# A softmax over relative-position-biased logits on one core: two reciprocals per chunk, and stores issued behind two exps of the next chunk

## Chip, core and metric

The kernel runs on one core of one Trainium2 chip. The metric is the device time of one execution in microseconds (us). Three executions of the kernel before took 1333.96, 1325.47 and 1325.87 us; the median is 1325.87 us.

## What is computed

The logits are a float32 array of 2 x 8 x 2112 x 2112, so there are 33,792 rows of 2112 numbers. To each row a bias is added that depends only on the head and on the distance of the two positions, clipped to 16 either way. Then each row goes through a softmax with its own maximum taken off.

```python
def reference(logits, rel_bias):          # (2, 8, 2112, 2112), (8, 33)
    rel = pos[:, None] - pos[None, :]
    rel_clipped = np.clip(rel, -16, 16) + 16
    logits = logits + rel_bias[:, rel_clipped][None]
    logits = logits - logits.max(axis=-1, keepdims=True)
    exp = np.exp(logits)
    return exp / exp.sum(axis=-1, keepdims=True)
```

## The kernel before

One partition of the 128 holds 132 consecutive rows of one batch. The work is cut into **chunks** of R = 6 rows per partition (128 x 12672 floats, one load and one store of 6336 KB each), and four chunks make a **round**: chunks 0 and 1 are twelve rows of the first batch, chunks 2 and 3 the same twelve of the second. There are K = 11 rounds, so 44 chunks. Four buffers `X[0]` to `X[3]` in on-chip memory hold one chunk each; chunk m of every round uses `X[m]`, and all work on it is done in place. In this document chunk (k, m) is chunk m of round k, counted from 0.

Each of three engines runs its own list of instructions in the order in which it is written, without a scheduler, and they meet at semaphores:

- **SP** issues the loads (`load`, L90-L91). The four loads of round 0 go at once. The load of chunk (k+1, m) waits at L88 until the store of chunk (k, m) has landed (`st[m]`), since it goes into the same buffer.
- **DVE** copies a window of the bias table once per round (L172). For each chunk it waits for the load (`ld[m]`), then adds the bias to each of the six rows and takes the negated maximum in the same instruction (`add`, L186; each is followed by a short read of the accumulator, which signals `added`). Then it runs `scale` (L207-L213): it waits until all six exps are done (`expd`), forms six reciprocals of the sums in one instruction (L210, which signals `inv`), waits for it, and multiplies the first DV = 4 rows (L213, each signals `scaled`).
- **ACT** runs the six exps of a chunk (`exps`, L192-L200; ACTIVATE at L197, each after its own `added`, and a read of the accumulator behind it, which signals `expd`). Then `scale_rest` (L215-L220) waits for `inv` and multiplies the last two rows (L218). Then `store` (L93-L95) waits until all six rows are scaled and issues the store of the chunk.

So loads go out on SP's queue and stores on ACT's queue, both to the same set of 16 DMA engines. On ACT a store stands behind all of its own chunk's work and ahead of the next chunk's exps. The helper `take` (L87-L88) waits for a semaphore to reach n and takes n off; it is a row of its own in the trace at L88 (EVENT_SEMAPHORE). Where an instruction only waits (`wait_ge`), the wait is part of that instruction.

Of the kernel before, what the change touches and what calls it, by code (L numbers as in the profile page):

```python
# [15 lines left out]
def kernel(  # L16
# [6 lines left out]
    nc = tc.nc  # L23
# [10 lines left out]
    NBUF = 4  # L34
    R = 6
# [3 lines left out]
    assert K * G == RP  # L39
    SW = S + G - 1  # L40
    DV = 4

    io = ctx.enter_context(tc.tile_pool(name="io", bufs=1))
    X = [io.tile([P, R * S], FP32, tag=f"X{b}", name=f"X{b}") for b in range(NBUF)]
# [5 lines left out]
    tot = io.tile([P, NBUF * R], FP32, tag="tot", name="tot")  # L50
    rec = io.tile([P, NBUF * R], FP32, tag="rec", name="rec")
# [15 lines left out]
    def view(t, offset, dims):  # L67
        return bass.AP(tensor=t.tensor, offset=t.offset + offset, ap=[[list(t.ap[0])[0], P]] + dims)

    def rows(t, k, m):  # L70
        return bass.AP(
            tensor=t.tensor, offset=t.offset + (m // M) * (H * S * S) + (m % M) * R * S + k * (G * S), ap=[[RP * S, P], [1, R * S]],
        )

    with tc.tile_critical(no_gpsimd_drain=True):  # L75
# [3 lines left out]
        expd = nc.alloc_semaphore("expd")  # L79
        scaled = nc.alloc_semaphore("scaled")  # L80
        inv = nc.alloc_semaphore("inv")
        rb = nc.alloc_semaphore("rb")
        zero = nc.alloc_semaphore("zero")
        idx = nc.alloc_semaphore("idx")
# [2 lines left out]
        def take(eng, sem, n):  # L87
            eng.wait_ge(sem, n).then_inc(sem, -n)  # L88
# [4 lines left out]
        def store(k, m):  # L93
            take(nc.scalar, scaled, R)
            nc.scalar.dma_start(out=rows(out, k, m), in_=X[m][:, :]).then_inc(st[m], 16)  # L95
# [10 lines left out]
        v = nc.vector  # L106
# [6 lines left out]
        def settle():  # L113
# [9 lines left out]
            out=bass.AP(tensor=F2.tensor, offset=F2.offset, ap=[[Q * step, P // Q], [1, H * W]]),  # L123
            in_=bass.AP(tensor=rel_bias.tensor, offset=rel_bias.offset, ap=[[0, P // Q], [1, H * W]]),
# [15 lines left out]
        for o, n, s, op in ((eq, NB, q, ALU.is_equal), (lt, NB, q, ALU.is_lt), (hsel, H, h, ALU.is_equal),  # L140
# [24 lines left out]
                           in_=view(reg, 1, [[1, NB - 1], [0, RP - W]])))  # L165
# [9 lines left out]
        def row(m, i):  # L175
            return X[m][:, i * S : (i + 1) * S]

        def col(t, m, i, n=1):
            c = m * R + i
            return t[:, c : c + n]  # L180
# [7 lines left out]
                    scale=-1.0, scalar=BIG, op0=ALU.add, op1=ALU.min, accum_out=col(nmax, m, i),  # L188
                ).then_inc(added, 1)

        def exps(m):
            for i in range(R):  # L192
                if i < R - 1:
                    nc.scalar.wait_ge(added, i + 1)
                else:
                    take(nc.scalar, added, R)
                nc.scalar.activation(  # L197
                    out=row(m, i), in_=row(m, i), func=ACTF.Exp, scale=-1.0, bias=col(nmax, m, i),
                    accum_out=col(tot, m, i),
                ).then_inc(expd, 1)  # L200

        def scales_begin(eng, m):
            if m < NBUF - 1:
                eng.wait_ge(inv, m + 1)
            else:
                take(eng, inv, NBUF)

        def scale(m):
            take(v, expd, R)
            v.reciprocal(out=col(rec, m, 0, R), in_=col(tot, m, 0, R)).then_inc(inv, 1 if m < NBUF - 1 else NBUF + 1)  # L210
            scales_begin(v, m)
            for i in range(DV):
                v.tensor_scalar_mul(out=row(m, i), in0=row(m, i), scalar1=col(rec, m, i)).then_inc(scaled, 1)  # L213

        def scale_rest(m):  # L215
            scales_begin(nc.scalar, m)
            for i in range(DV, R):
                nc.scalar.activation(  # L218
                    out=row(m, i), in_=row(m, i), func=ACTF.Copy, scale=col(rec, m, i),
                ).then_inc(scaled, 1)  # L220

        with nc.Fori(0, K, 1, engines=[ENG.DVE]) as k:  # L222
            window(k)
            for m in range(NBUF):
                add(m)
                scale(m)
        with nc.Fori(0, K, 1, engines=[ENG.Activation]) as k:
            for m in range(NBUF):
                exps(m)
                scale_rest(m)  # L230
                store(k, m)

# [28 lines left out]
```

## Time and profile before

| | before |
|---|---|
| median of three executions | 1325.87 us (1325.47 to 1333.96) |
| span of the profiled execution, first to last instruction | 1323.8 us |
| median less the span | 2.1 us |
| DVE busy, ACT busy | 866.2 us (65%), 757.2 us (57%) |
| bytes moved by DMA, mean rate over the span | 570.98 MB, 431 GB/s |
| queue of the loads (q1), queue of the stores (q10), share of 16 DMA engines | 50.0%, 49.8% |

The span is what the profiler recorded of one execution; no time of its own outside the span is given for that execution, so the 2.1 us are the difference to the median of the three. The page has a line for each engine with its busy time, a strip of 40 slices in which the DMA row tells how busy the 16 DMA engines were (9 is 90% or more), and the queues with their bytes. "Issue to landing" is the time from the instruction that starts a transfer to the last of its completion signals; it holds the time in which the transfer stands in a queue. A row of the timeline gives start, duration, engine, line and operation; in square brackets stands how long the engine idled before it, and what ended that. "DVEq" or "ACTq" is the part of an engine that handles waits and issues transfers. A transfer's end is seen as small packets of under 512 bytes, one from each of the 16 DMA engines.

### The profile page before, as it was taken

The page shows a single profiled execution, that of the slowest core. Times are in us where ns is not written, and L with a number is a line of the kernel's source. Part 1 is how long each engine was busy: PE and PEld are TensorE (multiplying, and loading weights), DVE is VectorE, ACT ScalarE, POOL GpSimd, SP SyncE. Part 2 cuts the span into 40 slices and gives each one's busy share as a digit, 9 for nine tenths or more (in the row PEclk, how much of TensorE's full clock was granted, in tenths as well). Part 3 has the DMA queues.
Part 4 walks back from the last instruction along what each step waited for, and adds up shares of the span by engine and source line. Part 5 has one row for each costly group of instructions (what it writes and reads, how often), then busy time and mean ns, then how long its engine had stood idle before and what let it go on. Part 6 is the DMA issues. An engine that isn't in the chain of part 4 may idle for free. (4 is left out here: it accounts for less than half of the span.)

```text
span 1323.8 us, 2109 instructions
## 1 busy us (share of the span) xinstructions
DVE 866.2 (65%) x781; ACT 757.2 (57%) x627; POOL 0.4 (0%) x6
## 2 busy tenths in 40 slices
DVE  6886666566766675576667666556766576566662
ACT  3776655556666555555656555555666565555663
POOL 0000000000000000000000000000000000000000
DMA  9999999999999999999999999999999999999998
GB/s 417 417 423 435 441 435 423 441 438 421 440 441 427 430 441 435 424 440 438 424 437 440 437 423 440 440 421 438 441 432 426 441 437 423 440 440 423 437 441 369
DMA packets 12682, 570.98 MB, mean 431 GB/s; under 512 B 1412, under 2 KB 1416, under 8 KB 1416
## 3 DMA queue, kind: packets, MB, share of 16 engines
q1 hardware_dynamic: 6336, 285.48, 50.0%
q10 hardware_dynamic: 6344, 285.48, 49.8%
q14 instruction: 2, 0.02, 0.0%
HBM read 285.48 MB, written 285.47 MB: 431 GB/s over the span
## 5 line engine op out<-in xcount | busy, mean ns | idle before, releaser
L197 ACT ACTIVATE X<-X,nmax 128x2112 f32<-128x2112 f32 x264 | 542.6, 2055 | 505.1 <-DVE nmax L186 472.4
L186 DVE CUSTOM_DVE_ANT_0 X<-X,F 128x2112 f32<-128x2112 f32 x264 | 605.2, 2354 | 319.1 <-DVEq L88 319.1
L213 DVE TENSOR_SCALAR X<-X,rec 128x2112 f32<-128x2112 f32 x176 | 220.3, 1315 | 2.8
L218 ACT ACTIVATE X<-X,rec 128x2112 f32<-128x2112 f32 x88 | 176.1, 2048 | 17.2 <-DVE rec L210 12.2
L210 DVE RECIPROCAL rec<-tot 128x6 f32<-128x6 f32 x44 | 8.4, 191 | 106.2 <-DVEq L88 106.2
L197 ACT ACTIVATION_READ_ACCUMULATOR X<-X,nmax 128x1 f32 x264 | 49.2, 186 | 0.0
L197 ACT ACT_TABLE_LOAD x11 | 14.1, 1283 | 22.6 <-ACTq L88 19.9
L172 DVE COPY F<-F 128x2123 f32 x11 | 26.0, 2361 | 0.5 <-DVEq L88 0.5
L186 DVE DVE_READ_ACCUMULATOR2_ANT nmax<- 128x1 f32 x264 | 21.6, 82 | 0.0
L144 DVE LOAD_MASK_SELECT F<-F x1 | 0.0, 14 | 6.2 <-DMA F<-in_rel_bias_dram 6.2
L164 DVE COPY F<-own 128x1485 f32<-128x1485 f32 x1 | 1.7, 1698 | 0.0
L120 DVE MEMSET F<- 128x264 f32 x1 | 0.3, 278 | 1.1 <-SPq L75 1.1
L142 DVE TENSOR_SCALAR Z<-rec,Z 128x16 f32<-128x16 f32 (+2 forms) x5 | 0.8, 233 | 0.1
L163 DVE TENSOR_TENSOR F<-F,own 128x528 f32<-128x528 f32 x1 | 0.7, 717 | 0.1
L160 DVE TENSOR_TENSOR F<-Z,own 128x528 f32<-128x528 f32 x1 | 0.7, 705 | 0.0
L150 DVE TENSOR_REDUCE own<-F 128x33 f32<-128x264 f32 x1 | 0.6, 609 | 0.1
L147 DVE TENSOR_TENSOR F<-F,Z 128x264 f32<-128x264 f32 x1 | 0.4, 429 | 0.1
L144 DVE STREAM_SHUFFLE F<-F 128x264 f32<-128x264 f32 x1 | 0.4, 442 | 0.0
L158 DVE SCALAR_TENSOR_TENSOR own<-Z,own 128x16 f32<-128x16 f32 x1 | 0.2, 235 | 0.2 <-DVEq L88 0.2
L155 DVE TENSOR_SCALAR own<-Z,own 128x16 f32<-128x16 f32 x1 | 0.2, 235 | 0.2 <-DVEq L88 0.2
L166 DVE COPY F<-own 128x115 f32<-128x115 f32 x1 | 0.3, 271 | 0.0
L168 DVE COPY F<-own 128x115 f32<-128x115 f32 x1 | 0.3, 271 | 0.0
(11 smaller groups left out, 1.6 us busy)
## 6 DMA issues: line engine op xcount, KB each, us to landing
X<-in_logits_dram SPq DMA_DIRECT2D x44, 6336.0 KB, 38.4
out_dram<-X ACTq DMA_DIRECT2D x44, 6336.0 KB, 59.0
F<-in_rel_bias_dram ACTq DMA_DIRECT2D x1, 4.1 KB
```

The source lines that it names most:

```text
L142: then(v.tensor_scalar(out=o, in0=num[:, 0:n], scalar1=s, scalar2=None, op0=op))
L144: then(v.stream_shuffle(out=T, in_=T, mask=[0] * Q))
L150: then(v.tensor_reduce(out=rbK, in_=view(F2, H * W, [[1, W], [W, H]]), axis=mybir.AxisListType.X, op=ALU.add))
L160: then(v.tensor_tensor(out=bands, in0=view(eq, 0, [[1, NB], [0, W]]), in1=view(rbK, W - 1, [[0, NB], [-1, W]]), op=ALU.mult))
L163: then(v.tensor_tensor(out=bands, in0=bands, in1=view(rest, 0, [[1, NB], [0, W]]), op=ALU.add))
L164: then(v.tensor_copy(out=view(F, C0 + W, [[RP, NB - 1], [1, RP - W]]), in_=view(reg, 1, [[1, NB - 1], [0, RP - W]])))
L172: then(v.tensor_copy(out=F2[:, 0:SW], in_=F[:, bass.ds(RP - G - k * G, SW)]))
L186: v.tensor_tensor_reduce(out=row(m, i), in0=row(m, i), in1=F2[:, x : x + S], scale=-1.0, scalar=BIG, op0=ALU.add, op1=ALU.min, accum_out=c ...
L197: nc.scalar.activation(out=row(m, i), in_=row(m, i), func=ACTF.Exp, scale=-1.0, bias=col(nmax, m, i), accum_out=col(tot, m, i),).then_inc( ...
L210: v.reciprocal(out=col(rec, m, 0, R), in_=col(tot, m, 0, R)).then_inc(inv, 1 if m < NBUF - 1 else NBUF + 1)
L213: v.tensor_scalar_mul(out=row(m, i), in0=row(m, i), scalar1=col(rec, m, i)).then_inc(scaled, 1)
L218: nc.scalar.activation(out=row(m, i), in_=row(m, i), func=ACTF.Copy, scale=col(rec, m, i),).then_inc(scaled, 1)
```

## The change

The change does two things.

The reciprocals are formed in two parts. DVE waits for the first four exps of the chunk (`wait_ge(expd, DV)`), forms four reciprocals, waits for them, and multiplies rows 0 and 1. Then it waits for all six exps, forms the other two reciprocals (signal `inv2`), and multiplies rows 2 and 3. ACT waits for `inv2` in place of `inv`, and multiplies rows 4 and 5 as before.

The store of chunks 0, 1 and 2 of a round moves on ACT behind the first AHEAD = 2 exps of the round's next chunk. The store of chunk 3 stands where it stood, right behind its own chunk's work, ahead of the next round.

```diff
+    AHEAD = 2
...
+        inv2 = nc.alloc_semaphore("inv2")
...
-        def exps(m):
-            for i in range(R):
+        def exps(m, a, b):
+            for i in range(a, b):
...
+        def scale_one(m, i):
+            v.tensor_scalar_mul(out=row(m, i), in0=row(m, i), scalar1=col(rec, m, i)).then_inc(scaled, 1)
 
         def scale(m):
+            v.wait_ge(expd, DV)
+            v.reciprocal(out=col(rec, m, 0, DV), in_=col(tot, m, 0, DV)).then_inc(inv, 1)
+            take(v, inv, 1)
+            for i in range(DV // 2):
+                scale_one(m, i)
             take(v, expd, R)
-            v.reciprocal(out=col(rec, m, 0, R), in_=col(tot, m, 0, R)).then_inc(inv, 1 if m < NBUF - 1 else NBUF + 1)
-            scales_begin(v, m)
-            for i in range(DV):
-                v.tensor_scalar_mul(out=row(m, i), in0=row(m, i), scalar1=col(rec, m, i)).then_inc(scaled, 1)
+            v.reciprocal(out=col(rec, m, DV, R - DV), in_=col(tot, m, DV, R - DV)).then_inc(inv2, 1)
+            for i in range(DV // 2, DV):
+                scale_one(m, i)
 
         def scale_rest(m):
-            scales_begin(nc.scalar, m)
+            take(nc.scalar, inv2, 1)
...
             for m in range(NBUF):
-                exps(m)
+                exps(m, 0, AHEAD)
+                if m:
+                    store(k, m - 1)
+                exps(m, AHEAD, R)
                 scale_rest(m)
-                store(k, m)
+            store(k, NBUF - 1)
```

ACT's list before, from the first chunk's exps on; X_58 is the buffer of chunk 0 and X_59 that of chunk 1, and "ISA [waits scaled]" is the start of the store at L95:

```order
L197 ACTIVATE X_58,tot<-X_58,nmax 128x2112 [waits added] x6
L218 ACTIVATE X_58<-X_58,rec 128x2112 [waits inv]
L218 ACTIVATE X_58<-X_58,rec 128x2112
L95 ISA [waits scaled]
L95 DMA out_dram<-X_58 128x12672
L197 ACTIVATE X_59,tot<-X_59,nmax 128x2112 [waits added] x6
```

The same place after the change:

```order
L199 ACTIVATE X_58,tot<-X_58,nmax 128x2112 [waits added] x6
L221 ACTIVATE X_58<-X_58,rec 128x2112 [waits inv2]
L221 ACTIVATE X_58<-X_58,rec 128x2112
L199 ACTIVATE X_59,tot<-X_59,nmax 128x2112 [waits added] x2
L97 ISA [waits scaled]
L97 DMA out_dram<-X_58 128x12672
L199 ACTIVATE X_59,tot<-X_59,nmax 128x2112 [waits added] x4
```

The store of chunk 0 stands behind two exps that wait for the adds of chunk 1, and so for the load of chunk 1.

DVE's list before, at the end of chunk 0 (its last add, then `scale`, then the first add of chunk 1):

```order
L186 ISA X_58,nmax<-X_58,F_62 128x2112
L186 ISA nmax 128x1
L210 RECIPROCAL rec<-tot 128x6 [waits expd]
L213 TENSOR_SCALAR X_58<-X_58,rec 128x2112 [waits inv]
L213 TENSOR_SCALAR X_58<-X_58,rec 128x2112 x3
L186 ISA X_59,nmax<-X_59,F_62 128x2112 [waits ld1]
```

The same place after the change:

```order
L188 ISA X_58,nmax<-X_58,F_62 128x2112
L188 ISA nmax 128x1
L209 RECIPROCAL rec<-tot 128x4 [waits expd]
L205 TENSOR_SCALAR X_58<-X_58,rec 128x2112 [waits inv]
L205 TENSOR_SCALAR X_58<-X_58,rec 128x2112
L214 RECIPROCAL rec<-tot 128x2 [waits expd]
L205 TENSOR_SCALAR X_58<-X_58,rec 128x2112 x2
L188 ISA X_59,nmax<-X_59,F_62 128x2112 [waits ld1]
```

Two of the four multiplications moved ahead of the wait for the sixth exp, and there is one reciprocal more.

More of the change, by code (lines that the diff above doesn't have):

```diff
@@ L200, in exps @@
                 ).then_inc(expd, 1)
[L202 to L206, printed above, removed]
-        def scale(m):
+        def scale_one(m, i):
+            v.tensor_scalar_mul(out=row(m, i), in0=row(m, i), scalar1=col(rec, m, i)).then_inc(scaled, 1)
+        def scale(m):
+            v.wait_ge(expd, DV)
[3 more added lines that the diff above has]
+                scale_one(m, i)
             take(v, expd, R)
-            v.reciprocal(out=col(rec, m, 0, R), in_=col(tot, m, 0, R)).then_inc(inv, 1 if m < NBUF - 1 else NBUF + 1)
-            scales_begin(v, m)
-            for i in range(DV):
-                v.tensor_scalar_mul(out=row(m, i), in0=row(m, i), scalar1=col(rec, m, i)).then_inc(scaled, 1)
+            v.reciprocal(out=col(rec, m, DV, R - DV), in_=col(tot, m, DV, R - DV)).then_inc(inv2, 1)
+            for i in range(DV // 2, DV):
+                scale_one(m, i)
         def scale_rest(m):
-            scales_begin(nc.scalar, m)
+            take(nc.scalar, inv2, 1)
             for i in range(DV, R):
```

## Prediction

> **What bounds the kernel now.** I read the page's engines and queues first, to see whether any engine is full.
>
> ```profile
> span 1323.8 us, 2109 instructions
> DVE 866.2 (65%) x781; ACT 757.2 (57%) x627; POOL 0.4 (0%) x6
> DMA  9999999999999999999999999999999999999998
> ...
> q1 hardware_dynamic: 6336, 285.48, 50.0%
> q10 hardware_dynamic: 6344, 285.48, 49.8%
> ```
>
> No compute engine is over two thirds busy. The loads (q1) and the stores (q10) fill the 16 DMA engines to 99.8% of the span, in every slice of the strip. Second, the DMA view over windows: the steady part (60 to 1280 us), and the start (2 to 32 us), where only loads run.
>
> ```profile
> DMA packets 11753, 529.45 MB, mean 434 GB/s; under 512 B 1307, under 2 KB 1307, under 8 KB 1307
> ```
> ```profile
> DMA packets 278, 12.88 MB, mean 429 GB/s; under 512 B 20, under 2 KB 24, under 8 KB 24
> q1 hardware_dynamic: 270, 12.87, 100.9%
> ```
>
> The rate is 434 GB/s mixed, and 429 in a short window of loads alone with the engines just as full. So it matters little which queue has work, as long as one has. 570.96 MB (two times 285.48) at 434 GB/s are 1315.6 us. That leaves 8.2 us of 1323.8 in which the DMA engines are not at full rate, most of it at the very start and end. Third, the waits, and for the transfers the time from issue to landing.
>
> ```profile
> ACT X L197 <- DVE nmax L186: 472.4, 44, 17.2
> DVE X L186 <- DVEq L88: 319.1, 42, 8.5
> ```
> ```profile
> L91 SPq DMA_DIRECT2D X<-in_logits_dram x44: 332/333/549, 1.0 to 1244.2; - x44
> ...
> DMA to landing us min/median/max: 17.6/38.4/82.8
> ```
> ```profile
> L95 ACTq DMA_DIRECT2D out_dram<-X x44: 338/339/380, 40.4 to 1303.3; - x44
> ...
> DMA to landing us min/median/max: 19.3/59.0/60.5
> ```
>
> DVE waits some 7.6 us (319.1/42) for each load, and ACT waits behind DVE. The first pair of landing rows is the loads', the second the stores', each with the first and last issue. One transfer at full rate takes 6.488 MB / 434 GB/s = 14.9 us, yet a load takes 38.4 and a store 59.0: the rest is waiting in a queue that is never empty. Last, the timeline of one chunk and the begin of the next:
>
> ```profile
> 145.18 2.36 DVE L186 CUSTOM_DVE_ANT_0 X<-X,F 128x2112 f32<-128x2112 f32 x1 [8.49 <-DVEq L88]
> ...
> 156.37 0.19 ACT L197 ACTIVATION_READ_ACCUMULATOR X<-X,nmax 128x1 f32 x1
> ...
> 158.86 0.08 DVE L186 DVE_READ_ACCUMULATOR2_ANT nmax<- 128x1 f32 x1
> ...
> 161.03 0.19 ACT L197 ACTIVATION_READ_ACCUMULATOR X<-X,nmax 128x1 f32 x1
> 161.36 0.19 DVE L210 RECIPROCAL rec<-tot 128x6 f32<-128x6 f32 x1 [2.42 <-DVEq L88]
> 161.58 4.00 ACT L218 ACTIVATE X<-X,rec 128x2112 f32<-128x2112 f32 x2 [0.37 <-DVE rec L210]
> 161.59 5.01 DVE L213 TENSOR_SCALAR X<-X,rec 128x2112 f32<-128x2112 f32 x4
> ...
> 166.83 0.34 ACTq L95 DMA_DIRECT2D out_dram<-X  x1
> 175.08 2.36 DVE L186 CUSTOM_DVE_ANT_0 X<-X,F 128x2112 f32<-128x2112 f32 x1 [8.49 <-DVEq L88]
> ...
> 177.48 2.06 ACT L197 ACTIVATE X<-X,nmax 128x2112 f32<-128x2112 f32 x1 [11.90 <-DVE nmax L186]
> ...
> 179.76 2.05 ACT L197 ACTIVATE X<-X,nmax 128x2112 f32<-128x2112 f32 x1
> ...
> 181.72 0.19 ACT L197 ACTIVATION_READ_ACCUMULATOR X<-X,nmax 128x1 f32 x1
> ```
>
> A chunk takes 175.08 - 145.18 = 29.90 us, and a load and a store at full rate take 2 x 14.95 = 29.9. The period is the DMA's; compute fills 21.65 of it (145.18 to 166.83). A buffer's round trip is 38.4 + 21.8 + 59.0 = 119.2 us, four periods.
>
> **The change, part by part.** *The reciprocals.* One RECIPROCAL more per chunk costs at most 0.19 us (its row), 44 x 0.19 = 8.4 us of DVE. Its cover is DVE's wait for the next load, 8.49 us in this chunk. The first reciprocal needs four exps, done at 156.37 + 0.19 = 156.6, before DVE's own last add ends at 158.9: its wait is nothing. It runs from about 159.0 and two scales (5.01/4 = 1.25 us each) end at 161.8, after the sixth exp (161.2). Then the second reciprocal, and two scales end at about 164.6, against 166.6 before. ACT's two scales (4.00 us) start some 0.5 us later than 161.58, as they wait for the second reciprocal, and end near 166.1. So the chunk is scaled at 166.1 in place of 166.6: 0.5 us earlier on the way to a store, 2 us earlier on DVE. What DVE gains becomes a longer wait for the load, which the DMA sets: 0 us of the span. Without that cover the extra reciprocals would cost 8.4 us.
>
> *The stores of chunks 0 to 2* (33 of 44). Before, the store goes at 166.83. After, it stands behind two exps of the next chunk, which wait for its load and two adds. No row shows whether ACT issues the store when the second exp starts (179.76) or when it has ended (181.72 + 0.19 = 181.9), so the delay is 12.9 to 15.1 us. The transfer itself is not made longer; I take the delay as hidden, for this reason. The DMA engines run dry only if no buffer has a transfer in a queue. While store m is held back until some 5 to 7 us after load m+1 lands (175.08 to 179.8 or 181.9), the other two buffers' loads or stores are outstanding, and the load that lands next still has most of a period of DMA work ahead of it (loads land 29.90 us apart). In the round trip: 119.2 - 21.8 - 15.1 leaves 82 us for two transfers of 15, so the delay eats 15 of some 52 us of queueing. SP's wait for that store is no later than before, since the store stands that much less long in its queue: from 59.0 to 44 or 46 us. On ACT, the remaining exps now stand behind an issue of 0.34 us whose wait (`scaled`) is long met; ACT idles 11.9 us per chunk. Cost 0.
>
> *The tail* is the one place without other work, since loads have ended there. The last load lands just before the last add, and three stores remain. The rows are the last chunk's, then the landing of the single stores issued at 1243.3, 1273.4 and 1303.3 us, then the packets from 1281.6 to 1289.5 us.
>
> ```profile
> 1243.33 0.34 ACTq L95 DMA_DIRECT2D out_dram<-X  x1
> ...
> 1273.37 0.34 ACTq L95 DMA_DIRECT2D out_dram<-X  x1
> 1281.59 2.36 DVE L186 CUSTOM_DVE_ANT_0 X<-X,F 128x2112 f32<-128x2112 f32 x1 [8.54 <-DVEq L88]
> ...
> 1286.27 2.06 ACT L197 ACTIVATE X<-X,nmax 128x2112 f32<-128x2112 f32 x1
> ```
> ```profile
> out_dram<-X ACTq DMA_DIRECT2D x1, 6336.0 KB, 49.3
> ```
> ```profile
> out_dram<-X ACTq DMA_DIRECT2D x1, 6336.0 KB, 34.3
> ```
> ```profile
> out_dram<-X ACTq DMA_DIRECT2D x1, 6336.0 KB, 19.3
> ```
> ```profile
> DMA packets 64, 3.24 MB, mean 411 GB/s; under 512 B 0, under 2 KB 0, under 8 KB 0
> ```
>
> They land at 1292.6, 1307.7 and 1322.6, 15 us apart: back to back. After the change the store of chunk (10, 2) goes at 1286.3 (start of the second exp) to 1288.4 (its end, and 0.1 for the read) instead of 1273.4. It is late only if the store before it has left the DMA engines by then. At 1289.5 not one of the 16 had finished (no packet under 512 B); the last landed at 1292.6. How long a store takes from issue to its first packet has one case with the other queue full: issued at 40.4, no packet of q10 until 44.7, four by 46. Loads into an empty DMA at the start, issued from 1.0, had 16 packets by 3.0: 2 us at most.
>
> ```profile
> q1 hardware_dynamic: 32, 1.62, 112.0%
> ```
> ```profile
> q10 hardware_dynamic: 4, 0.20, 8.4%
> ```
> ```profile
> q1 hardware_dynamic: 16, 0.81, 120.1%
> ```
>
> So the first packets come between 1286.3 (no start at all) and 1292.7 (1288.4 and 4.3), against engines that come free between 1289.5 and 1292.6. The gap is from 0 to 3.2 us. I take 0: the short start is nearer, since no loads are queued there. The last chunk's own store, 0.5 us earlier than 1303.3, still waits for 1307.7: no gain.
>
> **Sum**: reciprocals 0, delay 0, tail 0 (to +3.2), so 1323.8 + 0 for the span, with the 2.1 us between span and median 1325.9 us, the median of before.
>
> **The rivals.** *The store is not delayed at all.* A wait belongs to the exp itself, and if ACT's sequencer goes on past an exp that still waits, it meets `scaled` and issues the store at about 166.3, where it did before. For it speaks that DVE's sequencer runs ahead of its engine, in the last rows of the chain:
>
> ```profile
> 1298.10 0.17 DVE X L213
> ...
> 1298.30 0.05 DVEq L222
> ...
> 1299.34 3.77 DVE X L213 x3
> ```
>
> The branch at L222 ran at 1298.30, with three scales in front of it still to run. No row shows it passing an instruction whose own wait is unmet. The Trainium skill, Perfetto Trace Analysis, section "Per-instruction lifecycle", says that a DVE or ACT instruction is pushed into a wait queue and the sequencer is then free to fetch the next; by that rule this rival would hold. The time is the same, 1325.9 us, with store landings near 59 us.
>
> *The delay is paid in the ring of buffers* (the other side). If a store's 59 us were its own time and not queueing, SP's wait for `st[m]` would end 13 us later each round, and ten rounds make 130 us: 1456 us. It decides if under 15 of the 52 us of queueing could be given back. Against it: the last store landed 15 us after the one before. The Trainium skill, DMA: Bandwidth & Descriptors, "Rules for kernel authors", advises to issue a DMA early; taken alone it speaks for this rival.
>
> *The tail gap*: 3.2 us, 1329.1 us, if the start takes 4.3 us there too.
>
> *Faster*: at most the 8.2 us outside full rate could go, and no row ties them to the moved instructions.
>
> **Numbers.** About 1% (1312.6 to 1339.1) is what a measurement of this kernel can tell from no change. Delay hidden 0.52, store not delayed 0.28, tail gap 0.10 are all within it: same 0.90. The ring, wholly or in part, is slower: 0.09. Faster 0.01, as 1312.6 is under 1315.6 at full rate. The range runs from 1322, a few us for a run without the small losses, over 1329.1 to 1334, the slowest run of before; only the ring is left out.
>
> **What would show it.** DMA at 434 GB/s from 60 to 1280 us, the chunk period 29.9 us; stores landing in a median of 44 to 46 us (hidden delay) or 59 (not delayed); RECIPROCAL x88, DVE's wait for loads up by about 2 us per chunk; in the tail three stores 15 us apart. A DMA rate under 434 in mid-span, or a period over 30 us, would prove me wrong.

## The result and the profile after

In 22 executions of each, the changed kernel took 1336.37 us (median; 1326.09 to 1338.95) and the kernel before 1327.23 us (1325.30 to 1336.83). The ratio of the comparison is 1.0038, 95% interval 1.002 to 1.0057: some 0.2 to 0.6% slower, within the 1% that was called "same". Median and ratio differ because both kernels have executions near 1326 us and near 1336 us: over 1333 us lie 15 of 22 of the changed kernel and 6 of 22 of before. The profiled execution of the changed kernel took 1336.1 us, with a span of 1334.3 us, and is of the longer sort; that of before (span 1323.8 us) is of the shorter. What follows compares these two, and explains the 10.5 us between them.

The page after, the same lines as those shown of before:

```profile
span 1334.3 us, 2219 instructions
...
DVE 864.5 (65%) x825; ACT 757.2 (57%) x627; POOL 0.4 (0%) x6
...
DMA  9999999999999999999999999999999999999977
...
q1 hardware_dynamic: 6336, 285.48, 49.7%
q10 hardware_dynamic: 6344, 285.48, 49.4%
```

The last two slices of the strip fell to 7: only there are DMA engines visibly idle. In mid-span, 60 to 1280 us, the rate is 433 GB/s against 434:

```profile
DMA packets 11723, 528.54 MB, mean 433 GB/s; under 512 B 1295, under 2 KB 1295, under 8 KB 1295
```

The waits and the two groups of reciprocals:

```profile
DVE X L188 <- DVEq L90: 431.5, 42, 11.7
```
```profile
L209 DVE RECIPROCAL rec<-tot 128x4 f32<-128x4 f32 x44 | 7.6, 173 | 0.0
L214 DVE RECIPROCAL rec<-tot 128x2 f32<-128x2 f32 x44 | 6.9, 157 | 0.0
```

The reciprocals no longer wait (0.0 idle before them, 106.2 us before the change), and DVE's wait for the loads took that time over: 319.1 us became 431.5 us. Both are off the path, as forecast.

The store of the second chunk of the last round, and the end of the run, in the timeline of ACT and DVE:

```profile
1267.02 2.06 ACT L199 ACTIVATE X<-X,nmax 128x2112 f32<-128x2112 f32 x1
1267.22 0.34 ACTq L97 DMA_DIRECT2D out_dram<-X  x1
...
1292.24 2.36 DVE L188 CUSTOM_DVE_ANT_0 X<-X,F 128x2112 f32<-128x2112 f32 x1 [10.83 <-DVEq L90]
...
1296.92 2.06 ACT L199 ACTIVATE X<-X,nmax 128x2112 f32<-128x2112 f32 x1
1297.13 0.34 ACTq L97 DMA_DIRECT2D out_dram<-X  x1
...
1313.22 0.34 ACTq L97 DMA_DIRECT2D out_dram<-X  x1
```

The store goes 0.20 us after the second exp has started (1267.02, 1267.22). So it is delayed as the text of the change says, and no further than to the start of that exp. The last load lands before 1292.24, where the last add begins; in before that was 1281.59. Where this lateness comes from is shown by a row of SP: the register instruction that runs between its wait for a store and the issue of the next load, from round 1 on. Its first and last start, in before and after:

```profile
L91 SPq FUSED_REGOPS  x40: 37/37/60, 75.7 to 1244.0; - x40
```
```profile
L93 SPq FUSED_REGOPS  x40: 37/37/60, 77.8 to 1254.7; - x40
```

From the first to the last of these 40 loads before took 1168.3 us, after 1176.9 us: 8.6 of the 10.5 us are lost in mid-run, and 2.1 at the start. From the last load's issue to the end of the span it is 79.6 us in before (1323.8 - 1244.2) and 79.4 us in after (1334.3 - 1254.9). The tail is no longer than it was, though it looks worse. The rate from 1290 to 1297.3 us, before and after:

```profile
DMA packets 65, 2.94 MB, mean 403 GB/s; under 512 B 7, under 2 KB 7, under 8 KB 7
```
```profile
DMA packets 15, 0.35 MB, mean 49 GB/s; under 512 B 8, under 2 KB 8, under 8 KB 8
```

In after, about two of the 16 DMA engines are at work there (49 of 434 GB/s), the rest have nothing to do. Engines that are done and one that is not: this leads to a quantity that the prediction did not consider. A transfer is cut into 16 shares, one for each DMA engine, and its end is the end of the last share. I call **spread** the time from the first to the last of a transfer's 16 completion packets (those under 512 bytes). For the first store of round 10 it is 4.0 us in before (1269.4 to 1273.4) and 22.5 us in after (1261.7 to 1284.2). The second last of the 16 is 7.4 us behind the first, so it is mostly one engine. In after the spread of the rounds' first stores grows: 2.2, 1.7, 3.4, 5.6, 9.0, 10.9, 12.7, 14.9, 18.6, 20.3, 22.5 us; in before 2.0 to 4.0 us.

How this sets the end is plain arithmetic. The last engine completes store (10, 1) and has two shares of 14.95 us left: 1302.9 + 29.9 = 1332.8, where the last completion of after is; 1292.2 + 29.9 = 1322.1 in before, measured 1322.2. The first engine completes store (10, 1) at 1289.8 in after and at 1289.6 in before. One engine has lost 10.7 us against before; the second last completes that store at 1293.6 in after and at 1290.4 in before, so the other fifteen have lost at most some 3 us.

The Trainium skill, DMA: Bandwidth & Descriptors, section "Why a DMA increments its semaphore by 16 and not by 1", says that a DMA runs on up to 16 engines that finish independently. The trace agrees: completions of store (10, 1) are 13.1 us apart.

Did the late engine run out of work in mid-run? The queues from 60 to 1280 us, before and after:

```profile
q10 hardware_dynamic: 5881, 264.85, 50.2%
q1 hardware_dynamic: 5871, 264.59, 50.1%
```
```profile
q10 hardware_dynamic: 5883, 265.00, 50.2%
q1 hardware_dynamic: 5839, 263.53, 50.0%
```

In both, the packets of the two queues fill all 16 engines (a little over 100%, since in the trace a packet begins some 4 ns before the one ahead of it ends). Counted packet by packet from 60 to 1260 us, the 16 engines together stand idle for 2.8 us in before and for 3.0 us in after. So the late engine always had work; the time was lost in packets that took longer.

### The profile page after: what moved, and what is told of

The parts are those of the page before. It is cut to its first block, busy times and chain, and to the rows that moved or that the text cites. A ratio compares the mean times of both kernels' runs of the same rounds, so it can differ in the third digit from the quotient of the medians.

```text
span 1334.3 us, 2219 instructions
## 1 busy us (share of the span) xinstructions
DVE 864.5 (65%) x825; ACT 757.2 (57%) x627; POOL 0.4 (0%) x6
## 5 line engine op out<-in xcount | busy, mean ns | idle before, releaser
L188 DVE CUSTOM_DVE_ANT_0 X<-X,F 128x2112 f32<-128x2112 f32 x264 | 605.2, 2355 | 431.5 <-DVEq L90 431.5
L205 DVE TENSOR_SCALAR X<-X,rec 128x2112 f32<-128x2112 f32 x176 | 223.0, 1312 | 6.6 <-DVEq L90 0.2
L209 DVE RECIPROCAL rec<-tot 128x4 f32<-128x4 f32 x44 | 7.6, 173 | 0.0
L214 DVE RECIPROCAL rec<-tot 128x2 f32<-128x2 f32 x44 | 6.9, 157 | 0.0
## 6 DMA issues: line engine op xcount, KB each, us to landing
out_dram<-X ACTq DMA_DIRECT2D x44, 6336.0 KB, 47.9
```

What stands on the lines that cost most here:

```text
L188: v.tensor_tensor_reduce(out=row(m, i), in0=row(m, i), in1=F2[:, x : x + S], scale=-1.0, scalar=BIG, op0=ALU.add, op1=ALU.min, accum_out=c ...
L209: v.reciprocal(out=col(rec, m, 0, DV), in_=col(tot, m, 0, DV)).then_inc(inv, 1)
L214: v.reciprocal(out=col(rec, m, DV, R - DV), in_=col(tot, m, DV, R - DV)).then_inc(inv2, 1)
```

## The experiments

Theories at the start: **tail gap** (the held store of the last round starves the DMA engines), **lag** (one engine falls behind over the rounds and sets the end by itself), **chance** (that lag is drawn in each execution, whatever the kernel). The first four kernels were:

**recip_only**: the stores go back to where they were.

```diff
-                exps(m, 0, AHEAD)
-                if m:
-                    store(k, m - 1)
-                exps(m, AHEAD, R)
+                exps(m, 0, R)
                 scale_rest(m)
-            store(k, NBUF - 1)
+                store(k, m)
```

> Two reciprocals, every store at once (no delay). Common to all theories: the DVE and ACT side of the change is covered by the wait for the loads, so the time is that of before, ratio 0.998 to 1.002, and the last completion of a store trails the first by 4 us or less at the end, as in before. If instead the ratio is over 1.003, the reciprocals are a part of the loss and the delay is not the only cause.

Measured: 1330.88 us median, ratio 1.0012 (0.9983 to 1.0041), spread 6.4 us, span 1327.4 us. The ratio fits, the spread is over the expected 4 us, and 3 of 12 executions are over 1333 us, against 10 of 35 of before beside it. The reciprocals are not shown to cost anything; a cost of up to 0.4% isn't excluded.

**delay_only**: before, with the stores of chunks 0 to 2 behind two exps.

```diff
+    AHEAD = 2
...
-        def exps(m):
-            for i in range(R):
+        def exps(m, a, b):
+            for i in range(a, b):
...
-                exps(m)
-                scale_rest(m)
-                store(k, m)
+                exps(m, 0, AHEAD)
+                if m:
+                    store(k, m - 1)
+                exps(m, AHEAD, R)
+                scale_rest(m)
+            store(k, NBUF - 1)
```

> One reciprocal as in before, stores of chunks 0 to 2 behind two exps of the next chunk. Theory tail gap (the held store of the last round leaves DMA engines without work) and theory lag (over the rounds one of the 16 DMA engines falls behind, from 2 us to 22 us between first and last completion of a store, and sets the end): the whole loss is here, ratio 1.003 to 1.007. Theory chance (the lag is drawn anew in each execution, whatever the kernel): ratio 0.998 to 1.002.

Measured: 1332.24 us, ratio 1.0025 (0.9998 to 1.0051), no execution of 12 under 1330 us, 5 over 1333 us. The profiled one has a spread of 7.9 us that stood from the first rounds on. It fits neither number well: inconclusive by itself, on the side of a loss.

**last_at_once**: the changed kernel, with the stores of round 10 alone at once (ACT's round is written out a second time behind a loop of K - 1, with 0 for a store right behind its chunk).

```diff
-        with nc.Fori(0, K, 1, engines=[ENG.Activation]) as k:
...
+        with nc.Fori(0, K - 1, 1, engines=[ENG.Activation]) as k:
+            round_act(k, AHEAD)
+        round_act(K - 1, 0)
```

> The changed kernel with the stores of the last round alone at once, the other ten rounds delayed. Theory tail gap: no engine runs dry after the last load, the time is that of before, ratio 0.998 to 1.002. Theory lag: the late engine has been falling behind for ten rounds and is still last, ratio 1.003 to 1.007, with a spread of 10 us or more between the first and last completion of the last round's first store.

Measured: 1336.72 us, ratio 1.0045 (1.0019 to 1.007), spread 22.5 us, 11 of 12 executions over 1333 us. The rate from 1290 to 1303 us, and the landing of store (10, 1), issued at 1253.83:

```profile
DMA packets 127, 5.63 MB, mean 433 GB/s; under 512 B 16, under 2 KB 16, under 8 KB 16
```
```profile
out_dram<-X ACTq DMA_DIRECT2D x1, 6336.0 KB, 50.0
```

The DMA engines are now full where they were at 49 GB/s, and the span is 1334.9 us all the same. The last engine completes store (10, 1) at 1303.5, and 29.9 us on is 1333.4, the measured end. **Tail gap** falls as the cause here: the gap is there in after, and costs nothing while one engine is later than it.

**after_again**: no edit.

> The changed kernel once more, for its spread from execution to execution and a second profile. Theory tail gap: the idle time of the DMA engines after the last load's first completion is 8 us again whatever the lag. Theory lag and theory chance: a profiled execution near 1326 us has completions within 5 us of each other at the end, one near 1336 us has over 15 us; the time goes with the lag. Ratio to before 1.003 to 1.007.

Measured: 1337.35 us, ratio 1.0024 (0.9993 to 1.0054); 8 of 12 executions are over 1333 us. The ratio is under the forecast 1.003, and its interval holds 1. The profiled execution, 1337.35 us, has a spread of 23.3 us, as **lag** forecast. **Chance** is right in part: over all comparisons 24 of 109 executions of before are over 1333 us, so the long executions come without the change too; of the changed kernel, with this run, it is 23 of 34. The change makes them more frequent.

The trace of after held one more difference. The very first store goes at 42.7 us, against 40.4 in before, so fewer loads are left in the queue when loads and stores begin to share the engines. I call **load margin** the first completion of a load less the issue of the next: 5.9 us in round 1 of before, 2.3 us in after. Theory **start** said that this alone brings the lag; **steady delay** said that all the delays do. Four kernels:

**first_store_at_once** and **first_store_late** (ACT's round 0 written out ahead of the loop; the four values tell which stores are delayed). The diff is of the first; the second has (True, False, False, False) for round 0 and four times False in the loop.

```diff
...
+        round_act(0, (False, True, True, False))
+        with nc.Fori(0, K - 1, 1, engines=[ENG.Activation]) as k:
+            round_act(k + 1, (True, True, True, False))
```

> The changed kernel, but the very first store, that of chunk (0, 0), goes at once; all other stores of chunks 0 to 2 stay delayed. Theory start: the only delay that counts is the first, since it sets how many loads are left in the queue when loads and stores begin to share the DMA engines; the margin of the loads (first completion of a load less the issue of the next) is 2.3 us in the changed kernel against 6.0 in before, and a load queue that runs empty lets one DMA engine fall behind. It expects a first store near 39.6 us, a load margin of 5 us or more, a spread of the last round's first store under 10 us and a ratio of 0.998 to 1.003. Theory steady delay: 32 delayed stores make the same loss as 33, ratio 1.004 to 1.007, spread over 15 us, margin near 2.3 us.

Measured: 1330.44 us, ratio 1.0011 (0.9986 to 1.0037), load margin 9.8 us, spread 5.9 us, 3 of 12 executions over 1333 us (8 of 35 of before beside it). This is what start forecast; **steady delay** falls, since its 1.004 to 1.007 lies outside the interval.

> Two reciprocals and every store at once, but the very first store, that of chunk (0, 0), goes behind two exps of chunk 1. Theory start: one delayed store of 44 brings the whole loss: first store near 42.7 us, load margin 2 to 3 us, spread over 10 us at the end, ratio 1.004 to 1.007. Theory steady delay: one store is nothing, time as with two reciprocals alone, ratio 0.999 to 1.003, spread of 6 us or less.

Measured: 1327.03 us, ratio 0.9977 (0.9956 to 0.9999), load margin 2.3 us, spread 7.9 us, no execution over 1328.92 us. The load margin is as small as in the changed kernel, and nothing is lost: **start** falls as the whole cause.

**ahead1** and **ahead4**: `AHEAD = 1` and `AHEAD = 4` in place of 2.

> The changed kernel with the stores behind one exp in place of two (AHEAD = 1). Theory start: the first store goes 2.3 us earlier, near 40.4 us as in before, so the load margin is near 5 us and the time that of before, ratio 0.998 to 1.003. Theory steady delay: the stores are still 11 us late, ratio 1.003 to 1.006.

Measured: 1326.20 us, ratio 0.9983 (0.9959 to 1.0007), load margin 6.4 us, spread 6.1 us, 1 of 12 over 1333 us. Stores some 11 us late cost nothing, against steady delay once more.

> The changed kernel with the stores behind four exps (AHEAD = 4). Theory start: the first store goes 4.6 us later, near 47 us, the load margin falls to zero or below, one DMA engine falls behind from the first rounds on, ratio 1.005 or more. Theory steady delay: 18 us of delay, more than with two exps: ratio 1.006 to 1.01. In the tail the store of chunk (10, 2) goes some 10 us after the last load in place of 5, so engines run dry for some 10 us; if that is on the path beside the lag, 1.008 or more.

Measured: 1337.09 us, ratio 1.0051 (1.002 to 1.0082), spread 22.6 us, reached by round 5 (22.2), 9 of 12 over 1333 us. The loads' first and last wait:

```profile
L93 SPq FUSED_REGOPS  x40: 37/37/60, 81.1 to 1257.0; - x40
```

Again the loss is there when the last load is issued (13.0 us after that of before), and the end follows 79.4 us later (span 1336.5 us). Twice the delay of the changed kernel's exps does not make more than the same spread.

What is left is that the changed kernel does not delay all stores. Stores go 16, 44, 30 and 30 us apart, since the fourth goes at once; in before all are 30 us apart. **Bunching** against **slack** (the time by which the next transfer already stands in its queue, summed over both queues):

**even_delay**: the fourth store is delayed like the others, behind two exps of the next round's first chunk (`before` is the number of the round ahead, none for round 0; the last line stands behind the loop).

```diff
...
                 exps(m, 0, AHEAD)
                 if m:
                     store(k, m - 1)
+                elif before is not None:
+                    store(before, NBUF - 1)
                 exps(m, AHEAD, R)
                 scale_rest(m)
-            store(k, NBUF - 1)
...
+        store(K - 1, NBUF - 1)
```

> The changed kernel with all four stores of a round delayed alike: the fourth goes behind two exps of the next round's first chunk, so stores are issued every 30 us instead of 16, 44, 30 and 30 us apart. Theory bunching (the uneven issue of stores throws the DMA engines out of step): no lag, ratio 0.998 to 1.003, spread under 8 us. Theory slack (what counts is how long the next transfer already stands in each queue before the first engine has finished the one ahead of it: 5.9 us for loads and 26 us for stores in before, 2.3 and 17 us in the changed kernel): the load's margin stays near 2 us and the stores' falls under 17 us, so the lag comes, ratio 1.004 or more, spread over 15 us.

Measured: 1326.69 us, ratio 1.0005 (0.9991 to 1.002), 1 of 12 executions over 1333 us. The page of even_delay, its rate from 60 to 1280 us, the landings, and the loads' waits:

```profile
span 1324.4 us, 2198 instructions
```
```profile
DMA packets 11756, 529.45 MB, mean 434 GB/s; under 512 B 1310, under 2 KB 1310, under 8 KB 1310
```
```profile
X<-in_logits_dram SPq DMA_DIRECT2D x44, 6336.0 KB, 34.7
out_dram<-X ACTq DMA_DIRECT2D x44, 6336.0 KB, 49.8
```
```profile
L93 SPq FUSED_REGOPS  x40: 37/37/60, 77.5 to 1246.4; - x40
```

Every store but the very last is delayed as in the changed kernel, the load margin is as small (2.9 us in round 1), the first load of round 1 is as late (77.5 us), and yet the 40 loads take 1168.9 us, 0.6 us more than in before. The spread ends at 4.7 us. Slack had expected the lag here and falls; **bunching** had expected this. One limit: in this comparison none of 17 executions of before is over 1333 us, and the changed kernel was not run again beside it. The next kernel was, and 4 of its 6 executions are over 1333 us.

**first_at_once_ahead4**: first_store_at_once with `AHEAD = 4`.

> First store at once, all other stores of chunks 0 to 2 behind four exps (AHEAD = 4). Theory load margin (the lag needs a load queue that is near empty from the start): the first store goes at 39.6 us, the load margin starts near 9 us, the time stays near that with the first store at once and two exps, ratio 1.000 to 1.004, spread under 10 us. Theory slack (sum of both margins): the stores' margin falls from 12 to about 7 us, the sum to 17 us, under the 19 us of the changed kernel: lag, ratio 1.004 or more, spread over 15 us.

Measured: 1339.02 us median of 6, ratio 1.0084 (1.0058 to 1.0109). The profiled execution is one of the short ones, 1329.92 us with a spread of 5.5 us, so it does not show where the others lost their time. A large load margin (9.5 us) doesn't protect, so theory load margin falls. Slack had forecast the ratio here, but not that of even_delay.

This profile shows one more thing: with the engines in step, the tail gap is on the path. The last engine completes store (10, 1) at 1295.0 us, but store (10, 2) is issued only at 1295.6, and its first packets start at 1296.5. All 16 engines idle for 1.5 us, and the end comes 31.7 us after 1295.0 instead of 29.9.

**before_again** and **before_again2**: the kernel before, once more.

> The kernel before, once more with a profile. Its executions lie near 1326 us or near 1336 us. If the time follows the lag of one DMA engine whatever the kernel, an execution near 1336 us has a spread over 15 us in the last round's first store, and one near 1326 us has under 6 us.

> The same as the run ahead of it, one more execution: spread over 15 us if it is near 1336 us, under 6 us if it is near 1326 us.

Measured: 1325.64 us with a spread of 4.6 us, and 1325.38 us with 2.6 us. No execution of before near 1336 us was caught with a profile, so that those have the same lag is likely, not shown.

All profiles together (spread: first store of round 10, and end: last completion, both of the profiled execution; the other columns are of all executions of the kernel, in the last column with those of before beside it):

| kernel | stores issued evenly | spread, us | end, us | median, us | ratio | over 1333 us; of before |
|---|---|---|---|---|---|---|
| before | yes | 4.0 | 1322.2 | 1327.23 | 1 | 6 of 22 |
| before_again | yes | 4.6 | 1322.3 | 1325.64 | | 0 of 1; 0 of 17 |
| before_again2 | yes | 2.6 | 1322.0 | 1325.38 | | 0 of 1; 0 of 17 |
| even_delay | yes | 4.7 | 1322.7 | 1326.69 | 1.0005 | 1 of 12; 0 of 17 |
| first_store_late | yes, but the first | 7.9 | 1325.7 | 1327.03 | 0.9977 | 0 of 12; 8 of 35 |
| recip_only | yes | 6.4 | 1325.9 | 1330.88 | 1.0012 | 3 of 12; 10 of 35 |
| ahead1 | no | 6.1 | 1326.2 | 1326.20 | 0.9983 | 1 of 12; 8 of 35 |
| first_store_at_once | no | 5.9 | 1325.3 | 1330.44 | 1.0011 | 3 of 12; 8 of 35 |
| delay_only | no | 7.9 | 1327.8 | 1332.24 | 1.0025 | 5 of 12; 10 of 35 |
| changed kernel | no | 22.5 | 1332.8 | 1336.37 | 1.0038 | 15 of 22; 6 of 22 |
| after_again | no | 23.3 | 1334.1 | 1337.35 | 1.0024 | 8 of 12; 10 of 35 |
| last_at_once | no, but the last round | 22.5 | 1333.4 | 1336.72 | 1.0045 | 11 of 12; 10 of 35 |
| ahead4 | no | 22.6 | 1335.1 | 1337.09 | 1.0051 | 9 of 12; 8 of 35 |
| first_at_once_ahead4 | no | 5.5 | 1326.7 | 1339.02 | 1.0084 | 4 of 6; 0 of 17 |

The executions with a spread over 20 us end at 1332.8 us or later, those under 8 us at 1327.8 us or earlier. Medians are of 6 to 22 executions (one for before_again and before_again2). The kernels with 8 of 35 beside them ran on another chip than the other experiments. All four kernels with a ratio whose interval is above 1 issue their stores unevenly, with two exps of delay or more. Uneven issue alone is not enough: ahead1 and first_store_at_once, the latter with two exps of delay, issue unevenly too and are not shown to differ from before. So bunching is what the losing kernels have in common, and even_delay speaks for it as the cause; it is not shown to be the cause.

## Why the prediction was right, and where it failed

**The DMA bounds the kernel: right.** The rate in mid-span is 433 GB/s, and the result is within 1%. The median of 1336.37 us itself lies above the range's 1334; the predicted 1325.9 us times the ratio is 1330.9 us. The sum said 0 us of loss, so the 0.2 to 0.6% are not in it; they lie within the forecast because "same" allowed for 1%.

**The reciprocals cost nothing: right, as far as it could be told** (ratio 1.0012, 0.9983 to 1.0041). The two forms take 173 and 157 ns, so DVE spends 14.5 us on the two instead of 8.4 us on the one: 6.1 us more, of at most 8.4 forecast. The cover named, the wait for the loads, grew by 112.4 us or 2.6 us per chunk where "about 2 us" was said.

**The store is delayed: right, at the lower bound.** From the last completion of load (10, 1) to the store it is 35.5 us against 22.2 us: 13.3 us more, of 12.9 to 15.1. The rival "not delayed" falls with it. The Trainium skill (Perfetto Trace Analysis, section "Per-instruction lifecycle") says that the sequencer is free for the next instruction once one has been pushed into the wait queue, and the prediction read this as ACT's sequencer going on past waiting exps. Here it did not: the store follows the second exp's start by 0.20 us.

**The delay is hidden: right for an even delay; for the uneven one of the change, not in every execution.** The row of the stores in after:

```profile
L97 ACTq DMA_DIRECT2D out_dram<-X x44: 338/338/383, 42.7 to 1313.2; - x44
...
DMA to landing us min/median/max: 20.0/47.9/63.0
```

Stores land in 47.9 us instead of 59.0 (44 to 46 forecast), so the queue gave most of the delay back. even_delay delays every store and loses nothing that could be measured. The ring of buffers, the rival on the other side, would have cost 130 us and did not come: the loads of after are issued 8.6 us further apart in all.

**The tail: the step that failed.** "Not one of the 16 had finished" and the gap of 0 to 3.2 us rested on the profile of before, where the 16 engines stay within 4.0 us of each other. In after, one engine is 13.1 us behind the first at store (10, 1). The store of chunk (10, 2) then goes at 1297.1 instead of 1286.3 to 1288.4, and most engines do run dry. The short start that the prediction chose fits: the first packets of this store start at 1298.0, 0.8 us after its issue. The gap itself came onto the path only where the engines were more nearly in step (0.5 us in delay_only, 1.5 us in first_at_once_ahead4). But the term that was missing stands in mid-run, not in the tail: 10.7 us of one engine's time, lost before the last load was issued, and the sum had no term for an engine that falls behind. The forecast's own signs of being wrong were both seen, by little: the rate fell from 434 to 433 GB/s in mid-span, and the period is over 30 us, (1254.7 - 77.8)/39 = 30.18 us from load to load, against (1244.0 - 75.7)/39 = 29.96 us in before. They do not show another limit than the DMA: its engines were busy in mid-run, and one of them was behind.

**What stays open** is why one engine falls behind, and why more often in the changed kernel. The lost time lies in slower packets. In the trace, packets of full size normally take 1.87 us. Of those after 50 us, 1 takes over 1.95 us in before, 15 in even_delay, 40 in recip_only, 50 in first_store_at_once, 68 in ahead1, 86 in after, 125 in last_at_once, 181 in delay_only and 246 in ahead4; most are loads. The 86 of after take 23.5 us more than normal ones would, all engines taken together. So slow packets come in kernels with even stores too, and in delay_only they are many without one engine far behind (spread 7.9 us). What makes a packet slow was not found, and the records don't name a packet's engine. Nor is it explained why before itself has long executions.

## What to carry to other kernels

In a kernel whose DMA is full all the time, a delay of 13 us in every store can cost nothing that could be measured, as in even_delay, where the queues held work throughout. An even issue of transfers is the safer form: the kernels that lost here issued them unevenly, though not all that did lost. Where executions are of two sorts, count each: here the long ones went from 6 to 15 of 22. Read a transfer's end engine by engine: a mean rate of 433 GB/s and a strip of 9s hid an engine that was 11 us late. And before idle time in a tail is blamed, compare the last load's issue with that of the kernel before: here the whole loss of the profiled execution was there already.

## What the runs showed of the hardware that was not expected

- The 16 DMA engines can drift apart while all of them are busy. In after the last engine lost 10.7 us against before in eleven rounds, about 1 us per round of 120 us. The spread stopped growing near 22.5 us (after_again: 22.5 us from round 7 to 9, ahead4: 22.2 us from round 5).
- The end of an execution follows from the last engine's completion of the third last transfer: it came 29.9 to 30.0 us later in 12 of the 14 profiles. In delay_only it was 30.6 us and in first_at_once_ahead4 31.7 us; in both all 16 engines idled in between, for 0.5 and 1.5 us.
- A store issued on ACT behind an exp that waits follows that exp's start by 0.20 us; the exp's own run of 2.06 us is not waited for.
- With nothing queued ahead of it on most engines, a store's first packets start 0.8 us after its issue (1297.1 to 1298.0 in after); with the loads' queue full, the very first store took 4.3 us (40.4 to 44.7 in before).
